# A two-layer trunk: the second input product of each feed-forward pair as seven products, with weight sums made by adding transfers

## The chip, the cores and the metric

The kernel runs on one core of a Trainium2 chip. The core has five engines with queues of their own: TensorE (PE, matmuls into PSUM), VectorE (DVE), ScalarE (ACT), GpSimd (POOL) and SyncE (SP, which here only issues transfers). Each queue runs in order; engines wait for each other by semaphores. 16 DMA engines move data between HBM and the on-chip buffer. The metric is the device time of one execution in microseconds (us). Before the change it is 1288.16 us, the median of 3 runs (1286.86 to 1289.29).

## The reference

A trunk of two layers on 512 tokens of width 1024, in float32. Each layer mixes tokens (layer 0: a gated linear recurrence beside stick-breaking attention; layer 1: a matrix memory) and then applies a convolutional gated feed-forward network, which is the part that matters here:

```python
def conv_glu_ffn(h, w_in, conv_w, conv_b, w_out):
    u = jnp.matmul(h, w_in)                  # 1024 -> 2 x 2816
    a, g = jnp.split(u, 2, axis=-1)
    a = causal_dwconv(a, conv_w, conv_b)     # 3 taps along the tokens
    return jnp.matmul(jax.nn.gelu(a) * g, w_out)   # 2816 -> 1024

# in each layer, around both sub-layers (mod = silu(c) @ ada_w + ada_b, six parts):
h = rmsnorm(x, norm_g) * (1 + scale) + shift
x = x + gate * sublayer(h)
```

## The kernel before

**Layout and precision.** Activations stand with channels on the 128 partitions and the 512 tokens along the row. A float32 operand is split into a high part, rounded to a faster matmul type (`hi`), and the rest (`lo`); a product is three matmuls, hi x hi, hi x lo and lo x hi (`mm3`, L254). Weights come by DMA as a `raw` tile; `split_w` (L219) makes `hi` with a cast on ScalarE (L222) and `lo` with a subtraction on VectorE (L223). Loads are issued by SP in order and wait there until a raw buffer is free.

**The feed-forward network** (`ffn`, L1130). The 2816 columns of either factor are 22 blocks of 128. Two pairs of blocks (fi = 0 and 2) are done first, plainly, while the second half of the normalised input is still being made. That half needs an inverse norm, computed by GpSimd (`rstd_of`, L336) and transposed by TensorE (L340). Then `tokens_side` makes combinations of token halves and channel halves, and nine **sets** follow, fi = 4, 6, ... 20, of two blocks each.

**A set.** The factor a ("X") is done by the class `Seven`: the weights of two blocks (1024 x 256) are seen as 2 x 2 blocks of 512 x 128, the input as 2 x 2 of 512 channels x 256 tokens, and Winograd's form of Strassen's scheme replaces eight block products by seven. Each product is 4 x 3 matmuls of 256 columns. Sums of the products are kept in PSUM where possible (products 1, 6, 7, 4 add up in one buffer, 5 and 3 in another, 2 in a third), and intermediate values are copied out after each. The sums of weights are four VectorE operations a set (L1083 to L1088). The factor g ("Y") is done plainly: two tiles of 8 x 3 matmuls of 512 columns. `ORDER` gives the order of these jobs, `FETCH` and `LEAD` how many jobs ahead loads and splits are called for. After the last job of a set, `post` applies convolution, gelu and the product of both factors, and splits the result into `acts`.

**Output products** are done in groups of 4 or 6 blocks of `acts`, put into the sets fi = 6, 10 and 14 and behind the last one (`out_jobs`); each output tile ends with an update of x on VectorE (L385). The last four blocks are multiplied at the end in two token halves.

**The conditioning** of layer 1 is 48 dot products on VectorE (L169, 1024 elements a row, with a 512 KB load each); 24 of them run in the network of layer 0, called for by `take`, two after each pair or set.

The Tile scheduler sets each engine's order from the program's order, the buffers and its own priorities.

## Time and profile before

| what | value |
|---|---|
| median of 3 runs | 1288.16 us |
| the profiled execution, device time | 1288.47 us |
| its span, first to last instruction | 1286.7 us |
| TensorE busy | 1246.4 us, 6942 matmuls seen |
| VectorE busy | 917.6 us |
| ScalarE busy | 578.9 us |
| GpSimd busy | 113.7 us |
| bytes moved | 161.04 MB |

Busy time is read per engine; matmuls are pipelined, so the printed durations of neighbouring matmuls overlap and their starts tell the spacing. A wait is put down to what ended it. Idle time of an engine that nobody waits for costs nothing. A few per cent of matmul records are missing from the trace, so counts of matmuls in a stretch are slightly low. In names, `wa` and `wg` are weights of the two factors, `was` sums of them, `wd` output weights, `pp`, `u` and `v` copies and sums of products, `th` and `tl` token combinations, `nr` the inverse norm, `acc` and `mx` PSUM buffers.

### The profile page before, as it was taken

To read this page: it belongs to the slowest core of one execution; us is meant where nothing else is said; L and a number is where in the kernel's file an instruction comes from. 1 tells how busy PE (TensorE), PEld (TensorE's weight loads), DVE (VectorE), ACT (ScalarE), POOL (GpSimd) and SP (SyncE) were. 2 spreads that over 40 slices of the span, in tenths; PEclk is the share of its full clock that TensorE was granted. 3 is DMA by queue.
4 is the path that set the end of the run, shared out by engine and by line. 5 is a ranking of instruction groups with operands and counts; after the bars stand their busy time and mean duration, and the time that the engine had idled before them with its cause. 6 is when DMAs were issued, how large, how long until landed. Compare 5 with 4: busy or idle time off the path is not lost.

```text
span 1286.7 us, 18103 instructions
## 1 busy us (share of the span) xinstructions
PE 1246.4 (97%) x6942; PEld 1060.2 (82%) x6942; DVE 917.6 (71%) x1503; ACT 578.9 (45%) x1011; POOL 113.7 (9%) x199
## 2 busy tenths in 40 slices
PE   5999999999989999999999999999999999999997
PEld 4876788899878888888897777778988888888887
DVE  7845788857876776768776869776797475657665
ACT  4454323235452434344446674774455152525432
POOL 0021254400000000000000120221000000000000
PEclk9999999999999999999999999999999999999999
DMA  8823655422434343435423338522232332323211
GB/s 319 296 70 99 220 171 178 135 83 67 147 99 148 120 141 118 140 119 181 136 80 115 98 100 267 157 66 67 66 115 75 106 114 83 112 85 111 86 49 66
DMA packets 47078, 161.04 MB, mean 125 GB/s; under 512 B 5136, under 2 KB 7568, under 8 KB 46992
## 3 DMA queue, kind: packets, MB, share of 16 engines
q1 hardware_dynamic: 46992, 159.89, 38.8%
q8 instruction: 54, 0.88, 0.3%
q14 instruction: 32, 0.26, 0.1%
HBM read 157.77 MB, written 2.10 MB: 124 GB/s over the span
## 4 chain that ended last, share of the span: by engine, by line
PE 86%; DVE 5%; issue 3%; ACT 3%; DMA 2%; POOL 1%; SPq 0%; POOLq 0%; DVEq 0%; ACTq 0%
PE acc L255 13%; PE acc L256 13%; PE acc L257 13%; PE mx L255 5%; PE mx L256 5%; PE mx L257 5%; PE acc L1107 4%; PE acc L1108 4%; PE acc L1109 4%; PE acc L657 2%; PE mx L488 2%; PE mx L659 2%; PE acc L289 1%; PE acc L291 1%; PE acc L290 1%
## 5 line engine op out<-in xcount | busy, mean ns | idle before, releaser
L255 PE MATMUL acc<-hh,wg 128*128 128x512 f32 (+1 forms) x384 | 144.0, 376 | 1.2 <-DVE cv L1148 1.2
L256 PE MATMUL acc<-hl,wg 128*128 128x512 f32 (+1 forms) x384 | 144.4, 376 | 0.0
L257 PE MATMUL acc<-hh,wg 128*128 128x512 f32 (+1 forms) x384 | 144.1, 376 | 0.0
L169 DVE CUSTOM_DVE_ANT_0 adaraw<-adaraw,csb,par 128x1024 f32<-128x1024 f32 x96 | 123.0, 1293 | 4.3 <-DMA adaraw<-adaT 4.2
L256 PE MATMUL mx<-actl,wd 128*128 128x512 f32 x288 | 113.5, 394 | 0.0
L255 PE MATMUL mx<-acth,wd 128*128 128x512 f32 x288 | 112.8, 395 | 0.0
L257 PE MATMUL mx<-acth,wd 128*128 128x512 f32 x288 | 112.1, 394 | 0.0
L255 PE MATMUL acc<-hh,w 128*128 128x512 f32 x256 | 105.6, 412 | 0.0
L222 ACT CAST w<-wraw 128x1024 fp32r<-128x1024 f32 x68 | 71.2, 1051 | 68.5 <-PE acc L256 35.0
L257 PE MATMUL acc<-hh,w 128*128 128x512 f32 x256 | 101.9, 398 | 0.0
L256 PE MATMUL acc<-hl,w 128*128 128x512 f32 x256 | 101.7, 397 | 0.0
L223 DVE TENSOR_TENSOR w<-wraw,w 128x1024 fp32r<-128x1024 f32 x68 | 83.5, 1234 | 24.3 <-ACT w L222 14.6
L1107 PE MATMUL acc<-th,wa 128*128 128x256 f32 x288 | 83.3, 289 | 4.9 <-ACT th L1187 3.5
L222 ACT CAST wg<-wgraw 128x1024 fp32r<-128x1024 f32 x44 | 46.1, 1048 | 86.5 <-PE acc L1108 64.6
L385 DVE SCALAR_TENSOR_TENSOR x<-mx,mod,x 128x512 f32<-128x512 f32 x64 | 47.8, 749 | 52.1 <-PE mx L257 51.7
L255 PEld LDWEIGHTS acc<-hh,wg 128*128 128x128 f32 x384 | 72.1, 188 | 14.8 <-ACT wa L222 1.4
L257 PEld LDWEIGHTS acc<-hh,wg 128*128 128x128 f32 x384 | 72.0, 188 | 13.7 <-DVE wg L223 0.4
L1108 PE MATMUL acc<-tl,wa 128*128 128x256 f32 x288 | 81.7, 284 | 1.1 <-DVE tl L1188 1.1
L256 PEld LDWEIGHTS acc<-hl,wg 128*128 128x128 f32 x384 | 72.1, 188 | 12.3
L1109 PE MATMUL acc<-th,wa 128*128 128x256 f32 x288 | 81.4, 283 | 0.0
L336 POOL TENSOR_TENSOR nr<-nv,mhalf 128x2 f32<-128x2 f32 (+1 forms) x9 | 7.7, 854 | 815.4 <-ACT nv L334 815.4
L222 ACT CAST wa<-was 128x1024 fp32r<-128x1024 f32 x36 | 37.8, 1050 | 69.1 <-PE mx L256 29.8
(307 smaller groups left out, 3254.9 us busy)
## 6 DMA issues: line engine op xcount, KB each, us to landing
adaraw<-adaT SPq DMA_DIRECT2D x96, 512.0 KB, 4.4
wraw<-wflat SPq DMA_DIRECT2D x76, 512.0 KB, 4.2
waraw<-wflat SPq DMA_DIRECT2D x44, 512.0 KB, 3.7
wgraw<-wflat SPq DMA_DIRECT2D x44, 512.0 KB, 4.4
wdraw<-wflat SPq DMA_DIRECT2D x32, 512.0 KB, 3.8
x<-xT SPq DMA_DIRECT2D x8, 256.0 KB, 4.6
wdraw<-wflat SPq DMA_DIRECT2D x8, 256.0 KB, 2.7
outT<-fin SPq DMA_DIRECT2D x6, 256.0 KB, 2.4
```

The source lines that it names most:

```text
L169: return nc.vector.tensor_tensor_reduce(out=tile_, in0=tile_, in1=csb, scale=1.0, scalar=pc("ada_b", o), op0=ALU.mult, op1=ALU.add, accum_ ...
L222: nc.scalar.copy(hi, src)
L223: nc.vector.tensor_sub(lo, src, hi.bitcast(F32))
L255: nc.tensor.matmul(out, ah, bh, start=start, stop=False)
L256: nc.tensor.matmul(out, ah, bl, start=False, stop=False)
L257: nc.tensor.matmul(out, al, bh, start=False, stop=stop)
L385: nc.vector.scalar_tensor_tensor(x[j][:, sl], ps, g, x[j][:, sl], op0=ALU.mult, op1=ALU.add)
L488: nc.tensor.matmul(lps[:, c * 64:(c + 1) * 64].rearrange("p (b m) -> p b m", m=m), k[:, s], qu, start=True, stop=True)
L657: nc.tensor.matmul(vps[i], act[:, i * P:(i + 1) * P], wt_[:, 0:512], start=s0, stop=s1)
L1107: nc.tensor.matmul(ps, hi[:, ks], bh, start=first and kk == 0, stop=False, skip_group_check=True)
L1108: nc.tensor.matmul(ps, hi[:, ks], bl, start=False, stop=False, skip_group_check=True)
L1109: nc.tensor.matmul(ps, lo[:, ks], bh, start=False, stop=kk == 3, skip_group_check=True)
```

## The change

Both factors of every set, in both networks, are done by `Seven` (`PAIRS`); jobs of X and Y alternate in the order `TWO`. The sums of weights are no longer made by VectorE: a tile is loaded with plain blocks by SP, and further blocks are added onto it by transfers with `accum_op=add` that GpSimd issues. Product 5's tile takes one such transfer of two blocks, product 6's takes three (one block, two, two), each after the one before. Signs are turned so that only additions are needed, and the token combinations and copies follow. Tiles of products 1, 5, 6 have two buffers of their own each (`raw`, `pr`, `qw`), shared by X and Y; product 4's block has smaller ones. Output groups are (0,4), (4,4), (8,4), (12,4), (16,2), placed after the fourth job of the sets fi = 4, 8, 12, 16 and behind the last; the other five sets have none. `tokens_side` is called before the first set instead of inside the pair fi = 2. A conditioning column is taken after each output tile of groups 1 to 4 and nowhere else.

```diff
-    NW, NR, NS, NQ, NX, NA = 45, 4, 10, 2, 2, 2
+    NW, NR, NS, NQ, NA = 44, 2, 10, 2, 2
...
+    def load_blocks(tile_, at, i0, n, add=False):
+        o, m = at + i0 * P * T, n * P * T
+        eng = nc.gpsimd if add else nc.sync
+        eng.dma_start(tile_.rearrange("p (b c) -> p b c", b=n),
+                      wflat[o:o + m].rearrange("(b p c) -> p b c", b=n, p=P),
+                      **({"accum_op": ALU.add} if add else {}))
...
-    ORDER = ("X1", "X5", "X6", "X2", "X7", "Y0", "X3", "X4", "Y1")
-    OUT_AT, LEAD, FETCH = 3, 6, 9
+    TWO = ("X1", "Y1", "X2", "Y2", "X5", "Y5", "X6", "Y6", "X3", "X7", "Y7", "Y3", "X4", "Y4")
+    LEAD, STAGE = 5, 3
+    PAIRS = (True, True)
...
-                nc.vector.tensor_add(src[:, 0:T], a21, a22)
-                nc.vector.tensor_sub(self.s2, src[:, 0:T], a11)
...
+            return {
+                1: [lambda: start(1, 0, 2)],
+                5: [lambda: add(5, 2), lambda: start(5, 1, 2)],
+                6: [lambda: load_blocks(t[6][:, 0:T], self.at, 3, 1, True), lambda: add(6, 2), lambda: add(6, 1),
+                    lambda: start(6, 0, 2)],
+                4: [lambda: start(4, 3, 1)],
+            }
         def prep(self, n):
...
+            hi, lo = split_w(self.t[n], self.name)
+            for i, m in enumerate({1: (2, 1), 5: (7, 5), 6: (3, 6), 4: (4,)}[n]):
...
-        groups = ((0, 6), (6, 4), (10, 4), (14, 4), (18, 4))
+        groups = ((0, 4), (4, 4), (8, 4), (12, 4), (16, 2), (18, 4))
...
                         x_update(ps, layer, 1, cb * (cols // P) + s)
+                        if gi > 0:
+                            take(1)
...
+            sevens = {"X": Seven(w, fi * P, bs, "wa")}
+            if two:
+                sevens["Y"] = Seven(w, F + fi * P, bs, "wg")
...
-            set_jobs(fi, {6: 0, 10: 1, 14: 2}.get(fi))
-        out_jobs(3)
+            set_jobs(fi, {4: 0, 8: 1, 12: 2, 16: 3}.get(fi))
+        out_jobs(4)
```

How the instructions stand, at three places.

GpSimd's queue at the start of layer 0's network, before: `nr` is the inverse norm of either token half, `hr` the last work of layer 0's mixer. The norm of the second half follows that of the first, and the next row is already layer 1's.

```order
L445 TENSOR_TENSOR hr_2256<-hr_2256,mhalf 128x4
L336 TENSOR_TENSOR nr_2592<-nv_2590,mhalf 128x2
L336 TENSOR_TENSOR nr_2795<-nv_2793,mhalf 128x2
L336 TENSOR_TENSOR nr_5956<-nv_5954,mhalf 128x2
L950 MEMSET vc_6142 128x4
```

The same place now. `waraw` and `wgraw` from `wflat` are adding transfers, X's and Y's; the brackets name the queues waited for, DMAHW a load's landing, DMASW an add's.

```order
L459 TENSOR_TENSOR hr_2256<-hr_2256,mhalf 128x4 [waits Pool_49]
L350 TENSOR_TENSOR nr_2592<-nv_2590,mhalf 128x2 [waits Activation_49]
L206 DMA waraw_3145<-wflat 128x2x512 [waits DMAHW2_49,DMAHW4_49,DMAHW0_49,DMAHW6_49,DVE_49,Activation_49]
L206 DMA waraw_3140<-wflat 128x2x512 [waits DMAHW5_49,DMAHW7_49,DMAHW0_49,DVE_49]
L350 TENSOR_TENSOR nr_2799<-nv_2797,mhalf 128x2 [waits Activation_49]
L206 DMA waraw_3140<-wflat 128x2x512 [waits DMASW1_49]
L206 DMA waraw_3140<-wflat 128x512 [waits DMASW2_49]
L206 DMA wgraw_3148<-wflat 128x2x512 [waits DMAHW7_49,DMAHW1_49,DVE_49]
L206 DMA wgraw_3142<-wflat 128x2x512 [waits DMAHW2_49,DMAHW0_49,DVE_49]
L206 DMA wgraw_3142<-wflat 128x2x512 [waits DMASW5_49]
```

Two adding transfers now stand ahead of the second half's norm; in layer 1's network it is one.

GpSimd's queue for one set, fi = 10, now (before, it had nothing between the norms): tiles 4194 and 4210 are product 5's of X and Y, 4102 and 4144 product 6's.

```order
L206 DMA waraw_4194<-wflat 128x2x512 [waits DMAHW4_49,DMASW0_49,DVE_49]
L206 DMA wgraw_4210<-wflat 128x2x512 [waits DMAHW7_49,DMASW1_49,DVE_49]
L206 DMA waraw_4102<-wflat 128x2x512 [waits DMAHW2_49,DMASW5_49,DVE_49]
L206 DMA waraw_4102<-wflat 128x2x512 [waits DMASW2_49]
L206 DMA wgraw_4144<-wflat 128x2x512 [waits DMAHW5_49,DMASW7_49,DVE_49]
L206 DMA waraw_4102<-wflat 128x512 [waits DMASW3_49]
L206 DMA wgraw_4144<-wflat 128x2x512 [waits DMASW4_49]
L206 DMA wgraw_4144<-wflat 128x512 [waits DMASW6_49]
```

The third add of X (one block) stands behind Y's first and its own second; each of the four last rows waits for the landing of an earlier add.

VectorE's queue among the first output tiles of a group in layer 0, before, in set fi = 6: `x` rows end an output tile, L223 rows are `lo` parts of splits, ISA rows are conditioning columns.

```order
L385 SCALAR_TENSOR_TENSOR x_78<-mx_3549,mod,x_78 128x512
L223 TENSOR_TENSOR wd_3423<-wdraw_3420,wd_3422 128x1024
L385 SCALAR_TENSOR_TENSOR x_79<-mx_3569,mod,x_79 128x512
L223 TENSOR_TENSOR wd_3474<-wdraw_3471,wd_3473 128x1024
L223 TENSOR_TENSOR wd_3429<-wdraw_3426,wd_3428 128x512
L169 ISA adaraw_3445,mod<-adaraw_3445,csb,par 128x1024
L169 ISA mod 128x1
L169 ISA adaraw_3448,mod<-adaraw_3448,csb,par 128x1024
L169 ISA mod 128x1
L385 SCALAR_TENSOR_TENSOR x_80<-mx_3589,mod,x_80 128x512
L223 TENSOR_TENSOR wd_3501<-wdraw_3498,wd_3500 128x1024
L223 TENSOR_TENSOR wd_3480<-wdraw_3477,wd_3479 128x512
```

The same kind of place now, in set fi = 8: `waraw_3759` is the tile of X6 (L237 is the old L223, L399 the old L385).

```order
L399 SCALAR_TENSOR_TENSOR x_80<-mx_4030,mod,x_80 128x512
L169 ISA adaraw_4044,mod<-adaraw_4044,csb,par 128x1024
L169 ISA mod 128x1
L399 SCALAR_TENSOR_TENSOR x_81<-mx_4047,mod,x_81 128x512
L169 ISA adaraw_4061,mod<-adaraw_4061,csb,par 128x1024
L169 ISA mod 128x1
L237 TENSOR_TENSOR wa_4065<-waraw_3759,wa_4064 128x1024
L399 SCALAR_TENSOR_TENSOR x_82<-mx_4068,mod,x_82 128x512
L169 ISA adaraw_4082,mod<-adaraw_4082,csb,par 128x1024
L169 ISA mod 128x1
L399 SCALAR_TENSOR_TENSOR x_83<-mx_4085,mod,x_83 128x512
L169 ISA adaraw_4099,mod<-adaraw_4099,csb,par 128x1024
```

A column now follows each output tile, and X6's split, which frees that tile's buffer for the next set, stands behind the fourth of eight output tiles.

## Rows read from the trace of the kernel before

**Rows 1.** page, first part: busy us (share of span) xinstructions by engine

```profile
PE 1246.4 (97%) x6942; PEld 1060.2 (82%) x6942; DVE 917.6 (71%) x1503; ACT 578.9 (45%) x1011; POOL 113.7 (9%) x199
```

**Rows 2.** windows: us, busy us (instructions) by engine, clock, DMA share, GB/s

```profile
400.00:500.00 100.00, 100.00 (x554) 86.12 (x553) 69.37 (x95) 38.04 (x52) 0.00 (x0) 1.00 0.40 130
1195.70:1217.60 21.90, 21.90 (x136) 19.58 (x135) 13.82 (x18) 10.57 (x17) 0.00 (x0) 1.00 0.34 103
```

**Rows 3.** timeline, TensorE: start, us, engine, line, operation; ends of two runs

```profile
500.05 0.39 PE L257 MATMUL acc<-hh,wg 128*128 128x512 f32 x1
...
504.48 0.39 PE L255 MATMUL acc<-hh,wg 128*128 128x512 f32 x1
...
507.81 0.28 PE L1108 MATMUL acc<-tl,wa 128*128 128x256 f32 x1
...
508.98 0.28 PE L1109 MATMUL acc<-th,wa 128*128 128x256 f32 x1
```

**Rows 4.** timeline, ScalarE: copies of first products, sets 18 and 20

```profile
590.93 0.37 ACT L1113 COPY pp<-acc 128x256 f32<-128x256 f32 x1
...
612.07 0.37 ACT L1113 COPY pp<-acc 128x256 f32<-128x256 f32 x1 [0.17 <-PE acc L256]
```

**Rows 5.** groups by line: shapes xcount | busy us, mean ns | idle before

```profile
L169 DVE CUSTOM_DVE_ANT_0 adaraw<-adaraw,csb,par 128x1024 f32<-128x1024 f32 x96 | 123.0, 1293 | 4.3 <-DMA adaraw<-adaT 4.2
L223 DVE TENSOR_TENSOR wa<-was,wa 128x1024 fp32r<-128x1024 f32 x36 | 44.0, 1223 | 21.1 <-ACT wa L222 20.5
L223 DVE TENSOR_TENSOR wa<-waraw,wa 128x512 fp32r<-128x512 f32 x18 | 12.3, 685 | 0.0
L385 DVE SCALAR_TENSOR_TENSOR x<-mx,mod,x 128x512 f32<-128x512 f32 x64 | 47.8, 749 | 52.1 <-PE mx L257 51.7
L1121 DVE TENSOR_TENSOR v<-mx,pp 128x256 f32<-128x256 f32 x18 | 7.5, 418 | 1.3 <-PE acc L1109 1.2
L222 ACT CAST wg<-wgraw 128x1024 fp32r<-128x1024 f32 x44 | 46.1, 1048 | 86.5 <-PE acc L1108 64.6 <-PE acc L256 20.7 <-PE mx L1108 0.6
L1113 ACT COPY pp<-acc 128x256 f32<-128x256 f32 x18 | 6.6, 367 | 0.9 <-DVE actl L251 0.8 <-PE acc L256 0.2
```

**Rows 6.** TensorE's waits, 300:660 and 910:1287: total us, times, longest

```profile
PE acc L1107 <- ACT th L1187: 3.5, 1, 3.5
PE acc L1108 <- DVE tl L1188: 0.3, 1, 0.3
...
PE mx L340 <- POOL nr L336: 1.1, 1, 1.1
PE acc L1108 <- DVE tl L1188: 0.8, 1, 0.8
PE acc L1107 <- ACT pp L1113: 0.5, 1, 0.5
```

**Rows 7.** timelines, GpSimd and VectorE, norms at both networks' start

```profile
308.89 0.70 POOL L336 TENSOR_TENSOR nr<-nv,mhalf 128x2 f32<-128x2 f32 x1 [16.53 <-ACT nv L334]
...
922.34 0.70 POOL L336 TENSOR_TENSOR nr<-nv,mhalf 128x2 f32<-128x2 f32 x1 [17.94 <-ACT nv L334]
...
304.03 1.22 DVE L223 TENSOR_TENSOR wa<-waraw,wa 128x1024 fp32r<-128x1024 f32 x1
```

**Rows 8.** DMA, 5:30, then 400:600: GB/s by slice, issues, us to landing

```profile
GB/s 302 311 318 377 387 400 403 429 419 419 419 419 419 419 419 413 406 413 413 400 400 413 413 419 197 92 229 374 243 157 315 302 203 328 282 236 334 354 354 380
DMA packets 2774, 8.71 MB, mean 348 GB/s; under 512 B 308, under 2 KB 308, under 8 KB 2774
q1 hardware_dynamic: 2774, 8.71, 94.7%
...
wraw<-wflat SPq DMA_DIRECT2D x4, 512.0 KB, 6.3
...
wgraw<-wflat SPq DMA_DIRECT2D x14, 512.0 KB, 4.7
waraw<-wflat SPq DMA_DIRECT2D x12, 512.0 KB, 3.7
```

More of the change, by code (lines that the diff above doesn't have):

```diff
@@ new lines, in tokens_side @@
+            uh, u, vh, v = (wt(n, [P, 2, 256], dt=F32R) for n in ("th", "tl", "th", "tl"))
+            nc.scalar.copy(uh[:, 0, :], uf[:, 0, :])
+            nc.scalar.activation(uh[:, 1, :], uf[:, 1, :], AF.Identity, bias=ns)
+            nc.vector.tensor_sub(u[:, 0, :], uf[:, 0, :], uh[:, 0, :].bitcast(F32))
+            nc.vector.scalar_tensor_tensor(u[:, 1, :], uf[:, 1, :], ns, uh[:, 1, :].bitcast(F32), op0=ALU.add,
+                                           op1=ALU.subtract)
+            nc.scalar.copy(vh, vf)
@@ L1248, in post @@
             def post():
-                take(2)
                 for s in range(2):
-                    act_g(act_a(fi + s, first.v[s]), st[s])
-            order = FIRST if fi == 4 else ORDER
+                    act_g(act_a(fi + s, sevens["X"].v[s]), sevens["Y"].v[s] if two else st[s])
+            order = TWO if two else ONE_FIRST if fi == 4 else ONE
+            out_at = 4 if two else 3
+            base = len(jobs)
+            pos = {name: i for i, name in enumerate(order)}
             for i, name in enumerate(order):
-                if i == OUT_AT and outs is not None:
+                if i == out_at and outs is not None:
@@ L1256, in set_jobs @@
                     out_jobs(outs)
                 n = int(name[1])
-                p = PREPS[i] if i < len(PREPS) else None
                 prep = None
-                if p:
-                    prep = second_prep if p[0] == "Y" else lambda n=int(p[1]): first.prep(n)
-                jobs.append((first.fetch if i == 0 else None, prep,
-                             (lambda n=n: first.run(n)) if name[0] == "X" else lambda n=n: second(n),
-                             post if i == len(order) - 1 else None))
@@ L1266, in ffn @@
-        for fi in range(4, NF, 2):
-            set_jobs(fi, {6: 0, 10: 1, 14: 2}.get(fi))
-        out_jobs(3)
-        nf = npr = 0
-        for j, (_, _, run, post) in enumerate(jobs):
-            while nf < min(j + FETCH, len(jobs)):
-                if jobs[nf][0]:
-                    jobs[nf][0]()
-                nf += 1
+                if name[0] in sevens:
+                    sev = sevens[name[0]]
+                    if n in (1, 5, 6, 4):
+                        prep = seven_at(sev, n, len(jobs))
+                    run = lambda sev=sev, n=n: sev.run(n)
+                else:
+                    if n == 0:
+                        prep = second_prep
+                    run = lambda n=n: second(n)
@@ L1275, in ffn, with advance @@
+                jobs.append((prep, run, post if i == len(order) - 1 else None))
+        for fi in range(4, NF, 2):
+            set_jobs(fi, {4: 0, 8: 1, 12: 2, 16: 3}.get(fi))
+        out_jobs(4)
+        fetches.sort(key=lambda e: e[:2])
+        npr = 0
+        def advance(j):
+            nonlocal npr
+            while fetches and fetches[0][0] <= j:
+                fetches.pop(0)[2]()
             while npr < min(j + LEAD, len(jobs)):
-                if jobs[npr][1]:
-                    jobs[npr][1]()
+                if jobs[npr][0]:
+                    jobs[npr][0]()
@@ L1278, in ffn @@
                 npr += 1
+        for j, (_, run, post) in enumerate(jobs):
+            advance(j)
+            if j == 0:
+                for kk in range(4):
+                    tokens_side(kk)
             run()
```

123 lines of the change are left out of this document (65 added, 58 removed).

## The prediction

> **What bounds the kernel now.** The page comes first: TensorE is busy for 97% of a span of 1286.7 us, VectorE for 71%, ScalarE for 45%, GpSimd for 9% [rows 1]. A busy TensorE alone proves little, so the windows are read next. In 100 us of the first feed-forward network, and in a set of the second, TensorE shows no gap at the full clock (1.00, the 2.4 GHz level), while the DMA engines are busy for 0.40 and 0.34 of the time [rows 2]. The list of TensorE's waits closes it: from the norm of either network's input to its end the longest are 3.5 us, once, for the token combinations, and 1.1 us, once, for the norm [rows 6]. So in these stages the time is the number of matmuls times their spacing, as long as everything else stays hidden.
>
> The spacing is read from starts, since the printed durations overlap. With 512 columns, 20 consecutive starts run from 500.05 to 504.48: 4.43 us over 19 steps, 0.233 us each. With 256 columns, 11 starts run from 507.81 to 508.98: 0.117 us each [rows 3]. Halving the columns halves the step; the weight loads do not set a floor there. As a check, a set of two column pairs without output products goes from 590.93 to 612.07, 21.14 us [rows 4]; 48 x 0.233 + 84 x 0.117 is 21.0.
>
> **What the change takes away.** Each of 18 sets (nine in either network) did its second factor in 48 matmuls of 512 columns, 11.2 us; it now does seven products of 12 matmuls of 256, 84 x 0.117 = 9.83 us, or 9.95 if the 0.14 us that my sum is short in the set is put on the sevens. I take 9.9: a gain of 1.29 us a set, 23.2 us for 18. All of it is on the path. The token combinations are now needed only after the first two pairs of products and a group of output products (four jobs of 5.6 us, two tiles of 12 matmuls of 0.233), so the waits of 3.5, 0.3 and 0.8 us for them go: 4.6 us [rows 6]. The four VectorE sums of each old set were hidden under the matmuls and give no time back by themselves. The 24 conditioning columns stay in the first network, each now behind one output tile. There TensorE takes 2.8 us for a tile and VectorE 0.75 us to add it and 1.29 for a column [rows 5], 2.04 us; a split or two beside them is covered by the sets' loads being due later. I take nothing; without that cover it would be the columns' excess, 24 x 0.5 us at the most.
>
> **What it adds on VectorE and ScalarE.** A set without output products lasts 2 x 9.9 = 19.8 us now. Between 1195.7 and 1217.6 VectorE was busy for 13.8 us and ScalarE for 10.6 [rows 2]. Splitting fourteen blocks of 512 columns instead of nine costs VectorE 8.7 us (6 x 1.223 + 2 x 0.685) where it had 5.6, and three more product evictions cost 3 x 0.42 [rows 5]: 18.2 us of 19.8, 92%. ScalarE gets one wide and one narrow cast more and four evictions of 0.37: 13.7 us, 69%. Both still fit, but these queues run in order, and the slack of an eviction is short: the next set's first product takes the buffer whose last product was one job (1.4 us) earlier, and a cast of 1.05 us can stand in front of the copy of 0.37. In the old order the slack was as short in places (the product after X5 waits for X1's copy), and the second network's nine sets waited 0.5 us for such copies [rows 6]. So the cost lies between nothing and one such wait of 1.2 us a set, 22 us; nearest to the rows is a fraction, and with the fuller queues I take 0.3 us a set, 5 us in all.
>
> **What it adds at the start of each network.** GpSimd computes the inverse norms; in the first network it does so at 308.89 and in the second at 922.34, and TensorE waits 1.1 us for the latter [rows 6, 7]. Now two adding transfers stand in front of it in GpSimd's queue in the first network and one in the second, each waiting for a load whose buffer VectorE frees with a split such as those that end by about 305.3 [rows 7]. A load then lands 3.7 to 4.7 us later [rows 8], near 309.5, so the norm starts some 1 to 3 us late; TensorE's transposes of it, and with them all that it has queued behind, wait. Between nothing and two whole landings (9 us), I take 3 us for both networks.
>
> **What it adds to the transfers.** This is the term that no row shows: there is no adding transfer before. A block is 128 x 512 numbers, 0.262 MB. A seven loads seven blocks and adds seven, in four adding transfers; it loaded four before. X6's chain is one load, two adds of 0.52 MB and one of half that, each after the one before it has landed, and Y6's runs beside it, interleaved on GpSimd's queue. The tile of X6 is freed by its split in the fourth of eight output tiles, 11.2 us before the set goes on; the next set's split is due after ten more products less two, so 11.2 + 11.3 = 22.5 us later if that set has no output products. Five of nine sets are like that; the others have some 39 us. With a load of 4.2 us [rows 8] and L for an add, a shorter one at L - 1, X6 is ready at 4.2 + 3L - 1, which allows L up to 6.4 us. Y6's load starts two output tiles (5.6 us) later and its split is due at about 26 us: 9.8 + 3L - 1, so L up to 5.7. From below L is 3.7 us, a plain load; from above 12.6, two passes of the 6.3 us that a load takes when the engines are full [rows 8]. I take 5.5: a plain load of 4.2 us and 1.3 us for a second pass of 0.52 MB at the 400 GB/s of a full stretch. That leaves 0.6 us in each of ten sets; with some spread I take 3 us in all. The first set is loaded during 45 us of earlier products.
>
> **The sum.** The profiled execution took 1288.47 us around its span of 1286.7; the median of the three runs is 1288.16, so it stands for them. -23.2 - 4.6 + 5 + 3 + 3 = -16.8 us: 1271.7, and I predict 1272 us. What belongs to this case alone is 1262 (no stall at all, 1288.5 - 27.8 = 1260.7, and a little left) to 1278 (evictions 11 us instead of 5).
>
> **Rival on the other side: adds that pass their bytes twice fill the DMA engines.** Nine sets of 19.8 us and output products for eighteen rows of weights at 5.6 us make 279 us, 31.0 us a set. A set moves 3.67 MB of loads, 3.67 of adds, 1.05 of output weights and, in the first network, 1.4 of conditioning rows: 9.8 and 8.4 MB, 316 and 271 GB/s. Counting adds double it is 13.5 and 12.1 MB, 435 and 390 GB/s. The fullest stretch moved 348 GB/s at a share of 94.7%, that is 368 at all of it, with whole slices above 400 [rows 8]. At 368 a set takes 36.7 and 32.9 us, 5.7 and 1.9 too long, 68 us over 18 sets; at 410 it is 32.9 and 31.0, 17 us. So 1289 to 1340, middle 1310, and slower as soon as more than 17 us is lost. Against it: at one pass the same engines have room in both networks. For it: an add has two operands to fetch where a load has one, and no row says that the second comes free.
>
> The Trainium skill, Collectives: The Full Stack, section The bandwidth ceiling, states this of a reduction between cores: it runs at half a copy's rate not because the addition is slow but because two sources are read through the same ring. By that rule this rival would be the result. No run here shows it yet for an add that ends in the state buffer.
>
> **Rival between: only the chain is late.** L is 6.3 to 7.2 us, for GpSimd's time to issue a transfer or its queue held by one late landing. Y6 is then 1.8 to 4.5 us late in ten sets; some 2 us of it pass unseen, since its products come two or more jobs after the split: 0 to 25 us, on average 11, in place of the 3 above: 1280 (1278 to 1290). The rest of the gain shows, but TensorE has a regular gap in the sets without output products. GpSimd is idle in the networks, which speaks against a long writing time; four landings in series on one queue speak for it.
>
> **Rival: no gain in the matmuls.** If the sevens ran at the weight load's pace TensorE would gain nothing; the 0.117 us of the old sevens [rows 3] says no, and I give it no chance of its own.
>
> **How the numbers follow.** The forecast's case 52%, the late chain 20%, full DMA engines 25%, and 3% for faster than 1262. About 0.2% (2.6 us) is what a measurement tells from no change, so faster means below 1285.6: 52 + 3 and half of the late chain, 65%; same 8% (the end of the late chain and the start of the full engines); slower 27%. The range takes the late chain whole and half of the full engines: 1262 to 1312.
>
> **What would show it.** Right: matmul steps of 0.117 us through whole sets without output products, some 20 us from set to set; TensorE's share in the networks at 98% or more; adds that land within 6 us; VectorE near 90% in such sets. Wrong in the last terms: casts of the X6 and Y6 tiles on ScalarE waiting for a DMA, and TensorE idle behind evictions queued after them; DMA share near 1.0 through the first network but not the second (full engines), or moderate shares with long landings (late chain); a norm at the start of a network that waits for GpSimd's queue. If the sets take 20 us and the time still does not fall, the loss is at the start of the networks or in a stage that the change does not name, and the forecast's picture is wrong.

## The result, and the profile after

The changed kernel takes **1436.49 us** (median of 4 runs, 1433.98 to 1440.57): 1.1155 times the kernel before, with an interval of 1.1137 to 1.1172. The forecast was 1272. The profiled execution has a span of 1438.9 us. First its busy line, which answers to [rows 1]:

```profile
PE 1264.2 (88%) x7590; PEld 1105.0 (77%) x7590; DVE 932.4 (65%) x1537; ACT 630.4 (44%) x1123; POOL 278.4 (19%) x343
```

TensorE's idle time, span less busy, was 1286.7 - 1246.4 = 40.3 us and is 174.7 now. Its busy time should have fallen by the 23 us that the matmuls are worth and has risen by 17.8. So some 134 us are waits, and some 40 us are matmuls at a lower clock (e7 below has the same number of matmuls, busy for 1225.2 us at a clock of 1.00). The windows show both (us, busy us of PE, PEld, DVE, ACT and POOL, granted clock, DMA share, GB/s), the first one against the same stretch in [rows 2]:

```profile
400.00:500.00 100.00, 81.39 (x528) 74.98 (x529) 61.84 (x86) 39.10 (x64) 22.82 (x20) 0.89 0.95 236
470.00:480.00 10.00, 2.33 (x18) 2.12 (x18) 3.47 (x5) 0.20 (x1) 2.30 (x3) 0.86 1.05 283
480.00:490.00 10.00, 4.06 (x19) 4.06 (x20) 3.18 (x4) 2.48 (x4) 1.69 (x3) 0.50 0.87 201
560.00:570.00 10.00, 0.00 (x0) 0.00 (x0) 0.00 (x0) 0.00 (x0) 2.10 (x2) 0.63 0.94 221
570.00:580.00 10.00, 8.21 (x52) 8.21 (x53) 5.52 (x8) 5.49 (x9) 4.60 (x4) 0.69 0.91 174
```

The DMA share is 0.95 where it was 0.40. In 560:570 no engine but GpSimd does anything, and GpSimd only issues adds: the kernel waits for transfers. After such a gap TensorE comes back at a lower clock: 0.50, its 1.2 GHz level, in 480:490, and 0.69 in 570:580. Who waits for what is in the lists of waits (total us, times, longest). TensorE's, in the first and in the second network:

```profile
PE acc L1125 <- ACT wg L236: 66.3, 8, 14.0
...
PE acc L1125 <- ACT wg L236: 45.0, 8, 9.2
```

ScalarE's, over the whole span:

```profile
ACT wa L236 <- DMA waraw<-wflat: 107.9, 10, 15.6
```

TensorE's 111.3 us are waits for casts of the second factor's tiles, ScalarE's 107.9 us waits of casts of the first factor's for transfers. One such place in ScalarE's timeline (start, us, engine, line, operation, idle time before it):

```profile
570.17 1.04 ACT L236 CAST wa<-waraw 128x1024 fp32r<-128x1024 f32 x1 [14.93 <-DMA waraw<-wflat]
571.12 0.61 ACT L236 CAST wg<-wgraw 128x512 fp32r<-128x512 f32 x1
```

And in TensorE's:

```profile
571.79 0.58 PE L1125 MATMUL acc<-th,wg 128*128 128x256 f32 x1 [13.84 <-ACT wg L236]
```

In ScalarE's order the narrow cast (Y4, the last product of the running set) stands right behind the cast of the tile with three adds, X6 of the next set. ScalarE stops for X6, and TensorE for Y4, whose own tile is a plain load. The transfers over the sets of the first network, 340:700, with queue totals (packets, MB, share of 16 engines) and medians from issue to landing, against [rows 8]:

```profile
q0 software_dynamic: 15616, 29.88, 49.5%
q1 hardware_dynamic: 21270, 51.41, 41.9%
...
wgraw<-wflat POOLq DMA_DIRECT2D x25, 512.0 KB, 9.1
waraw<-wflat SPq DMA_DIRECT2D x24, 512.0 KB, 5.5
wgraw<-wflat SPq DMA_DIRECT2D x24, 512.0 KB, 8.4
waraw<-wflat POOLq DMA_DIRECT2D x24, 512.0 KB, 9.0
```

q0 carries the adds: 58% of the bytes of q1 in more engine time. On the page of the whole execution, the second row being the adds:

```profile
q1 hardware_dynamic: 70608, 188.21, 39.3%
q0 software_dynamic: 34560, 66.07, 27.5%
```

188.21 MB in 39.3% of 16 x 1438.9 us is 20.8 GB/s an engine, 333 on all; 66.07 MB in 27.5% is 10.4, or 167. Per byte, an add takes about twice the engine time of a load. The matmuls themselves keep the forecast's step; ten starts of TensorE in the changed kernel, 496.29 to 497.36, are nine steps of 0.119 us against 0.117 in [rows 3]:

```profile
496.29 0.28 PE L1127 MATMUL acc<-th,wg 128*128 128x256 f32 x1
...
497.36 0.28 PE L1127 MATMUL acc<-th,wg 128*128 128x256 f32 x1
```

And GpSimd at the start of the first network, where [rows 7] had the inverse norm at 308.89:

```profile
306.05 1.41 POOL L206 DMA_DIRECT2D waraw<-wflat  x1 [14.08 <-DVE hraw L392]
308.47 1.21 POOL L206 DMA_DIRECT2D waraw<-wflat  x1 [1.01 <-DVE hl L395]
309.24 1.19 POOL L350 TENSOR_TENSOR nr<-nv,mhalf 128x2 f32<-128x2 f32 x1
```

Two adds stand in front of it now, and it comes 0.35 us later.

### The profile page after: what moved, and what is told of

The parts are those of the page before. It is cut to its first block, busy times and chain, and to the rows that moved or that the text cites. A ratio compares the mean times of both kernels' runs of the same rounds, so it can differ in the third digit from the quotient of the medians.

```text
span 1438.9 us, 20091 instructions
## 1 busy us (share of the span) xinstructions
PE 1264.2 (88%) x7590; PEld 1105.0 (77%) x7590; DVE 932.4 (65%) x1537; ACT 630.4 (44%) x1123; POOL 278.4 (19%) x343
## 3 DMA queue, kind: packets, MB, share of 16 engines
q1 hardware_dynamic: 70608, 188.21, 39.3%
q0 software_dynamic: 34560, 66.07, 27.5%
## 4 chain that ended last, share of the span: by engine, by line
PE 48%; DMA 22%; DVE 11%; issue 10%; ACT 5%; POOL 3%; SPq 0%; POOLq 0%; DVEq 0%; ACTq 0%
DMA waraw<-wflat 7%; PE acc L269 7%; PE acc L270 7%; PE acc L271 7%; DMA wdraw<-wflat 7%; DMA wgraw<-wflat 6%; PE acc L1125 2%; PE mx L269 2%; DMA adaraw<-adaT 2%; PE mx L270 2%; PE acc L1127 2%; PE mx L271 2%; PE acc L1126 2%; PE mx L502 2%; PE acc L671 2%
## 5 line engine op out<-in xcount | busy, mean ns | idle before, releaser
L1125 PE MATMUL acc<-th,wg 128*128 128x256 f32 x288 | 88.2, 306 | 111.3 <-ACT wg L236 111.3
L236 ACT CAST wa<-waraw 128x1024 fp32r<-128x1024 f32 (+1 forms) x80 | 76.1, 952 | 211.1 <-DMA waraw<-wflat 107.9
L237 DVE TENSOR_TENSOR wa<-waraw,wa 128x1024 fp32r<-128x1024 f32 (+1 forms) x80 | 88.1, 1101 | 121.9 <-ACT wa L236 121.0
L206 POOL DMA_DIRECT2D waraw<-wflat x72 | 92.2, 1284 | 379.2 <-DMA waraw<-wflat 257.0
L1125 PEld LDWEIGHTS acc<-th,wg 128*128 128x128 f32 x288 | 59.0, 205 | 115.4 <-ACT wg L236 115.4
L206 POOL DMA_DIRECT2D wgraw<-wflat x72 | 95.9, 1332 | 248.1 <-DMA wgraw<-wflat 226.2
L169 DVE CUSTOM_DVE_ANT_0 adaraw<-adaraw,csb,par 128x1024 f32<-128x1024 f32 x96 | 123.8, 1294 | 26.1 <-DMA adaraw<-adaT 25.8
L269 PE MATMUL mx<-acth,wd 128*128 128x512 f32 x288 | 116.6, 408 | 8.6 <-ACT acth L264 5.5
L236 ACT CAST wg<-wgraw 128x1024 fp32r<-128x1024 f32 (+1 forms) x80 | 76.1, 952 | 74.4 <-PE mx L270 46.5
L269 PE MATMUL acc<-hh,w 128*128 128x512 f32 x256 | 105.2, 411 | 0.0
L237 DVE TENSOR_TENSOR wg<-wgraw,wg 128x1024 fp32r<-128x1024 f32 (+1 forms) x80 | 88.0, 1100 | 16.0 <-ACT wg L236 13.2
L237 DVE TENSOR_TENSOR w<-wraw,w 128x1024 fp32r<-128x1024 f32 x68 | 83.5, 1234 | 20.4 <-ACT w L236 10.9
L1127 PE MATMUL acc<-th,wg 128*128 128x256 f32 x288 | 85.2, 296 | 1.7 <-DVE wg L237 1.7
L1126 PE MATMUL acc<-tl,wg 128*128 128x256 f32 x288 | 85.2, 296 | 0.0
L399 DVE SCALAR_TENSOR_TENSOR x<-mx,mod,x 128x512 f32<-128x512 f32 x80 | 59.3, 748 | 38.6 <-PE mx L271 38.5
```

The costliest lines, as they stand in the source:

```text
L169: return nc.vector.tensor_tensor_reduce(out=tile_, in0=tile_, in1=csb, scale=1.0, scalar=pc("ada_b", o), op0=ALU.mult, op1=ALU.add, accum_ ...
L206: eng.dma_start(tile_.rearrange("p (b c) -> p b c", b=n), wflat[o:o + m].rearrange("(b p c) -> p b c", b=n, p=P), **({"accum_op": ALU.add} ...
L236: nc.scalar.copy(hi, src)
L237: nc.vector.tensor_sub(lo, src, hi.bitcast(F32))
L269: nc.tensor.matmul(out, ah, bh, start=start, stop=False)
L399: nc.vector.scalar_tensor_tensor(x[j][:, sl], ps, g, x[j][:, sl], op0=ALU.mult, op1=ALU.add)
```

## The experiments

The networks' times below run from the start of the inverse norm at a network's input to that of the first one after it, both on GpSimd. The forecast came to some 11 us less than before in the first and 8 in the second.

```
                                         us    ratio (interval)        1st net  2nd net
before                                 1288.2                           350.5    344.2
after                                  1436.5  1.1155 (1.1137-1.1172)   437.6    410.1
e1  adds as plain transfers            1332.6  1.0359 (1.0338-1.0380)   389.0    349.4
e2  adds of half the columns           1368.5  1.0638 (1.0613-1.0663)   391.8    379.3
e4  one seven, sums by adds            1300.5  1.0113 (1.0078-1.0148)   355.0    356.7
e6  one add a seven, VectorE the rest  1317.7  1.0246 (1.0229-1.0264)   368.1    353.3
e7  no sums                            1262.9  0.9810 (0.9796-0.9825)   336.5    334.7
e8  conditioning as before             1456.6  1.1296 (1.1268-1.1325)   456.5    409.0
e9  e6, second factor's by GpSimd      1362.6  1.0570 (1.0540-1.0599)   394.2    376.5
e10 e6, outputs meant to be even       1330.2  1.0329 (1.0313-1.0344)   378.9    357.5
e11 after, outputs meant to be even    1430.1  1.1088 (1.1052-1.1123)   439.6    394.0
e12 all sums on VectorE                1311.2  1.0178 (1.0163-1.0194)   362.4    353.9
e13 e12 in the second network alone    1291.9  1.0026 (1.0014-1.0038)   342.9    359.1
e14 one seven, all sums on VectorE     1279.8  0.9931 (0.9918-0.9945)   342.9    343.1
e15 e7, adds aside                     1546.0  1.2000 (1.1950-1.2050)   486.2    466.4
e16 e7, plain transfers aside          1415.5  1.0987 (1.0891-1.1083)   414.0    402.1
e18 after, product 4's tile elsewhere  1472.5  1.1445 (1.1419-1.1471)   450.8    422.5
```

**e1, e2: the adds' time on the engines.** e1 issues the same 144 transfers into the same tiles without the addition (the sums are left out); e2 adds half of the columns of each (half of the sums are left out).

```diff
-                      **({"accum_op": ALU.add} if add else {}))
+                      )
```

> The adding transfers are issued by GpSimd as plain transfers onto the same tiles (same count, size, queue and waits; the weight sums are left out). Theory A (an add takes two passes of the DMA engines, 10.4 GB/s an engine against 20.8, so the engines are full): a set then needs 29 us of the engines in the first network and 25 in the second, both under 31, so nearly all of the loss goes: 1270 to 1290 us, software queue's share near 14% instead of 27.5%. Theory B (the serial chain on GpSimd's queue is late whatever a transfer does): landings fall from 8 to some 5 us, but the queue's order stays and the sets stay long: above 1330 us.

> Each adding transfer moves only half of its columns (rows of 1 KB instead of 2; half of each weight sum is left out); count, order and waits as before. Theory A (bytes): the adds need 11 to 14 us of the engines a set instead of 22, so 25 to 32 us a set against 31: 1275 to 1310 us. Theory B (number of landings in series): the chain has as many landings, each 2 us or so of fixed time and most of the queueing kept, so the time stays above 1370 us.

The queue of these transfers in e1, then in e2:

```profile
q0 software_dynamic: 18432, 66.07, 14.7%
```

```profile
q0 software_dynamic: 34560, 33.04, 16.4%
```

In e1 the same bytes take 3131 engine-us, 21.1 GB/s an engine, in place of 6331, and 104 of the 148 us lost against the kernel before come back. So the doubled engine time, with what hangs on it, is most of the loss. (e1 also doubles the size of a packet and shortens GpSimd's issues, see the last section; no run takes these apart from the addition.) But it is not all: by its total e1 lies where theory B put it, above 1330 us, and 70 us above e7 below, which has no such transfers. Its landings (KB each, median us) and TensorE's wait for the second factor's casts:

```profile
waraw<-wflat POOLq DMA_DIRECT2D x54, 512.0 KB, 4.9
wgraw<-wflat POOLq DMA_DIRECT2D x54, 512.0 KB, 5.8
```

```profile
PE acc L1125 <- ACT wg L236: 34.5, 10, 10.6
```

The second network is nearly that of before (349.4); the first, where the conditioning loads come on top, is not. e2 lies between its two theories, just under B's 1370 us. It halves the bytes, but the packets stay as many, and one takes 0.104 us for 1 KB where an add of 2 KB took 0.183: halving a packet does not halve its time. Why e2's second network is 30 us behind e1's, at 3580 engine-us against 3131, is open; GpSimd's issues are as long in e2 as in the changed kernel (1.26 to 1.30 us), in e1 half that.

**e7: no sums at all.** Both factors as sevens in the new order with the new evictions; product 6 takes product 5's tile (the sums are left out).

```diff
-                5: [lambda: add(5, 2), lambda: start(5, 1, 2)],
-                6: [lambda: load_blocks(t[6][:, 0:T], self.at, 3, 1, True), lambda: add(6, 2), lambda: add(6, 1),
-                    lambda: start(6, 0, 2)],
+                5: [lambda: start(5, 2, 2)],
+                6: [lambda: same(6, 5)],
```

> Both factors as seven products, in the order and with the evictions of the change, but without any sum of weights: product 5 takes the second pair of blocks as it lies in memory, product 6 the same tile, so no adding transfer is issued and 5 blocks are loaded per seven where the changed kernel loads 7 and adds 7 (the sums are left out of the computation). Theory (the loss is in making the sums): with the sums gone the forecast's other terms must show, -23 us for matmuls, -5 for token combinations, +5 for evictions: 1262 to 1275 us, sets of 24 us without and 41 us with output products in both networks, no long wait of TensorE for a cast. Rival (the sevens themselves cost more than forecast, in splits on VectorE, evictions or buffers): 1285 us or more, with waits of TensorE on VectorE or ScalarE, not on transfers.

1262.93 us, at the lower end. Its busy line:

```profile
PE 1225.2 (97%) x7590; PEld 1075.9 (85%) x7590; DVE 932.2 (74%) x1537; ACT 630.2 (50%) x1123; POOL 114.3 (9%) x199
```

A window inside each network, as above:

```profile
400.00:590.00 190.00, 188.32 (x1295) 173.65 (x1294) 154.48 (x217) 93.36 (x144) 0.00 (x0) 1.00 0.58 183
1020.00:1210.00 190.00, 189.61 (x1319) 175.45 (x1318) 127.15 (x169) 93.66 (x147) 0.00 (x0) 1.00 0.34 110
```

ScalarE's copies of the first products of three sets:

```profile
398.02 0.64 ACT L1133 COPY pp<-acc 128x256 f32<-128x256 f32 x2
420.12 0.64 ACT L1133 COPY pp<-acc 128x256 f32<-128x256 f32 x2
461.65 0.64 ACT L1133 COPY pp<-acc 128x256 f32<-128x256 f32 x2
```

Busy time falls by 21.2 us (forecast 23.2 for the matmuls), idle time by 4.5; sets take 22.1 and 41.5 us at the full clock. All of the forecast but the sums is there. What is left, 1436.5 - 1262.9 = 174 us, is the price of making sums by adding transfers, with the two further blocks that each seven loads for them; the forecast had 3 us for it, and 3 for the norm behind the adds. Of the 174 us 104 go in e1 and 70 stay.

**e8: the conditioning columns as before**, two behind each pair and set instead of one behind an output tile.

```diff
                         x_update(ps, layer, 1, cb * (cols // P) + s)
-                        if gi > 0:
-                            take(1)
...
             def post():
+                take(2)
```

> The changed kernel with one part undone: the conditioning columns of the first network are taken as before (two behind each of the first tile pairs and behind each set) instead of one behind each output tile. Theory (transfer engines full): the conditioning bytes are the same, so the first network still lasts about 437 us and the whole 1425 to 1445 us. Rival (order of the queue: each conditioning load stands in SyncE's queue in front of weight loads and waits for its buffer there): the first network comes down toward the second's 410 us, the whole to 1405 to 1420 us.

Both missed: the first network gets slower by 19 us, the second stays. The change's placement is itself a gain where transfers are short; it is not part of the loss.

**e4, e6, e9, e12: the sums elsewhere.** e4 keeps the plain second factor (PAIRS is False twice) and makes one factor's sums by adds. e6 keeps both sevens and the adding transfer for product 5; product 6's sum is two VectorE additions. In e9 the second factor's two are GpSimd's; in e12 there is no adding transfer, and VectorE makes all sums.

```diff
             if n == 6:
+                t = self.t
+                s = t[6] = raw_tile(self.name + "s", D, "qw")
+                nc.vector.tensor_add(s, t[1], t[5])
+                nc.vector.tensor_add(s[:, 0:T], s[:, 0:T], t[4])
```

> The second factor again plainly, in 48 matmuls of 512 columns; the first factor's seven products with sums by adding transfers, the new groups and the new place of the conditioning columns stay. Theory A: per set 5.3 MB of plain loads and 1.84 MB of adds, 27 us of the engines in the first network, 23 in the second, of 32.3: it fits, so the time is that of before within a few us, 1285 to 1295. Theory B: one chain of four landings a set instead of two interleaved; by it too the sets fit, unless sets without output products (21 us) are late: 1290 to 1310.

> Both factors as seven products, but only product 5's sums by an adding transfer (one a seven instead of four); product 6's sums by two VectorE additions from the tiles of products 1, 5 and 4, which stay longer. Theory A: 5.1 MB of loads and 1.05 MB of adds a set, 21 us of the engines in the first network and 17 in the second, of 31: the engines have room, and the matmul gain of 23 us shows unless VectorE (3.8 us more a set) is the next bound: 1268 to 1290. Theory B: the chain is one landing long: the same, 1268 to 1290. If it stays far above 1290, what costs is neither the bytes nor the chain but the sevens themselves.

> The version in which only product 5's sums are made by an adding transfer and product 6's by two vector additions (1317.7 us), with the second factor's two additions on GpSimd instead of VectorE. If VectorE's share (81% in the first network, 68% in the second, and 17 us of TensorE's waits end on its split of the first factor) is what is left: 36 x 0.95 = 34 us off VectorE, TensorE's waits for it fall from 26 us toward 10 and the time to 1298 to 1308 us. If the queue order of loads and adding transfers is what is left, or GpSimd's additions (by the rows of 256 columns some 4 + 2 us a set) delay the adding transfers behind them: 1315 to 1330 us.

> Both factors as seven products in the change's order, but every sum of weights made by VectorE (four additions of 512 or two of 512 and one of 1024 columns a seven, 3.3 us) from the four blocks that each seven loads; no adding transfer at all. Without any sum the kernel takes 1262.9 us. VectorE gets 36 x 3.3 = 117 us more (932 to about 1050 us), and in a set without output products 18.2 + 6.6 = 24.8 us of work where the products take 19.8. Theory (the loss is the adding transfers' time on the transfer engines and the chain behind them; VectorE has the room on average): 1270 to 1295 us, below the 1317.7 us of the version with one adding transfer a seven. Rival (VectorE's bursts in the sets without output products bind, some 5 us late in each of ten sets and the clock lost behind each gap): 1305 us or more.

e4 halves the adds and keeps the matmuls of before, and is still 12 us slower than before: above what theory A allowed, inside B's range. e6 and e12 land between: 119 and 125 us better than the changed kernel, 30 and 23 worse than before. e6 misses both its theories (1268 to 1290 us); that the sevens themselves cost so much, which it names for that case, e7 rules out. Windows over the sets, e6 and then e12:

```profile
310.00:636.00 326.00, 304.08 (x2006) 277.90 (x2005) 261.98 (x374) 150.88 (x231) 20.86 (x18) 0.97 0.61 169
```

```profile
310.00:636.00 326.00, 308.36 (x2017) 278.88 (x2017) 285.79 (x415) 151.43 (x239) 0.69 (x1) 0.97 0.37 123
```

and TensorE's longest sum of waits in e12:

```profile
PE acc L1137 <- DVE wg L237: 16.1, 12, 2.0
```

In e12, with a DMA share of 0.37, VectorE is the late one: 88% busy over the window (80% in e6), and TensorE waits for its splits. e12's total is in its rival's range: the 25 us that e7 gains do not pay for VectorE's sums. e9 loses 45 us more than e6, outside both its ranges. Its GpSimd additions, and the wide and narrow splits of the first factor on VectorE beside them:

```profile
L1114 POOL TENSOR_TENSOR wgs<-wgraw,wgraw 128x1024 f32<-128x1024 f32 x18 | 52.9, 2939 | 259.3 <-DVE wd L237 139.0 <-ACT wa L236 55.1 <-DVE wg L237 26.3
...
L237 DVE TENSOR_TENSOR wa<-waraw,wa 128x1024 fp32r<-128x1024 f32 x44 | 57.9, 1317 | 0.5
L237 DVE TENSOR_TENSOR wa<-waraw,wa 128x512 fp32r<-128x512 f32 x18 | 17.7, 985 | 0.1
```

The narrow split takes 985 ns where it takes 685 [rows 5]: GpSimd's additions slow the engine that they were to relieve, and the adding transfers stand behind them in GpSimd's queue. What either costs of the 45 us is not separated.

**e10, e11: output products spread evenly.**

```diff
-            set_jobs(fi, {4: 0, 8: 1, 12: 2, 16: 3}.get(fi))
+            set_jobs(fi, {f: ((f - 4) // 4, (f - 4) // 2 % 2) for f in range(4, 20, 2)}.get(fi))
```

> The version with product 5's sums by one adding transfer and product 6's by two vector additions (1317.7 us), with the output products spread evenly: half a group behind every set instead of a whole group behind every second one, so a set is some 31 us throughout instead of 24 and 41 to 50. Theory (the limit is the rate of transfers and splits in the stretches without output products, since their mean over two sets is below TensorE's time: DMA share 0.66 and 0.52, VectorE 81% and 68%): TensorE's waits of 26 us and the clock lost behind them nearly vanish, 1270 to 1290 us, so at or below the kernel before. Rival (a chain of loads, adds and splits per set that is too long wherever it stands, or buffers held longer by the spread): 1305 us or more.

> The changed kernel with the output products spread evenly behind all sets in the same way. Theory (an add takes the transfer engines twice as long per byte, and the mean over two sets needs 40.4 us of them in the first network and 36.2 in the second where the products need 31): evening helps little, sets of 38 to 44 us throughout, 1400 to 1440 us. Rival (the series of four adding transfers is only late where a set without output products gives it 20 us): with 31 us for every set it fits (4.2 + 3 x 8 = 28 us), and the time falls to 1300 to 1350 us.

Neither tells anything of its question, though e10 lands in its rival's range and e11 in its theory's. First copies of three sets in e11:

```profile
417.53 0.64 ACT L1131 COPY pp<-acc 128x256 f32<-128x256 f32 x2
...
443.31 0.64 ACT L1131 COPY pp<-acc 128x256 f32<-128x256 f32 x2
...
504.02 0.64 ACT L1131 COPY pp<-acc 128x256 f32<-128x256 f32 x2
```

25.8 and 60.7 us: the sets are as uneven as they were, since TensorE got the output products of two sets nearly in one block whatever the order in the code: of their first matmuls (L269) 6 stand in the shorter stretch and 26 in the longer one, in e11 as in the changed kernel.

**e15, e16: the transfers without anyone who waits.** The kernel of e7, and beside it the changed kernel's adds (e16: plain transfers) into two tiles that nothing reads, with the load that starts each tile, from GpSimd's queue too. The sums stay left out.

```diff
-                5: [lambda: start(5, 2, 2)],
-                6: [lambda: same(6, 5)],
+                5: [lambda: add(9, 2), lambda: start(5, 2, 2)],
+                6: [lambda: (same(6, 5), load_blocks(t[9][:, 0:T], self.at, 3, 1, True)), lambda: add(9, 2),
+                    lambda: add(9, 1), lambda: start(9, 0, 2)],
```

> The version without sums (1262.9 us; six sets from the second to the eighth take 190.5 us in the first network and 189.0 in the second, in the changed kernel 259.5 and 235.6), with the changed kernel's adding transfers put back beside it: for every seven the same four adds (and the load that starts their tile, from GpSimd's queue too) go into a tile that nothing reads, so no product, load or split waits for an add; the two tiles for them turn on GpSimd's queue alone. The sums still don't enter the computation. Read from the pace of the sets, since GpSimd's late queue may hold the norm behind the network. Theory (the adds' time on the transfer engines makes the weight loads late): at the same bytes the six sets take 215 to 260 us with TensorE waiting for casts of loads, DMA share over 0.9. Rival (only the series of adds that a split waits for is late): the six sets stay at 189 to 197 us.

> The same with the transfers aside issued as plain ones, which take half the engine time per byte: both theories expect the six sets near 190 us (189 to 200); if they are as slow as with adds, it is the number of transfers and not their time on the engines that counts.

The six sets and the total can't be used: GpSimd's queue falls behind, and once in each network an output-weight load waits for it, some 120 us in e15. Before that stall there are two whole sets to read. e15's copies of first products:

```profile
408.06 0.64 ACT L1134 COPY pp<-acc 128x256 f32<-128x256 f32 x2
434.24 0.64 ACT L1134 COPY pp<-acc 128x256 f32<-128x256 f32 x2
483.29 0.64 ACT L1134 COPY pp<-acc 128x256 f32<-128x256 f32 x2
```

The window over them:

```profile
404.00:478.00 74.00, 66.91 (x424) 60.38 (x423) 50.44 (x71) 29.80 (x48) 18.45 (x17) 0.93 0.99 262
```

Landings of SyncE's loads in it (KB each, median us):

```profile
wgraw<-wflat SPq DMA_DIRECT2D x4, 512.0 KB, 7.9
...
waraw<-wflat SPq DMA_DIRECT2D x4, 512.0 KB, 8.9
```

The same loads in e7, 398:472:

```profile
waraw<-wflat SPq DMA_DIRECT2D x4, 512.0 KB, 4.7
wgraw<-wflat SPq DMA_DIRECT2D x4, 512.0 KB, 3.7
```

With nothing waiting for an add, the loads still land twice as late, and the pair of sets takes 75.2 us against 63.6 in e7 and 85.4 in the changed kernel (413.17 to 498.59). So in that pair 11.6 of 21.8 us come with traffic that nobody waits for. In the second network, before the stall, the same pair takes 67.0 us against 62.8 in e7 and 78.9 in the changed kernel: 4.2 of 16.1. The rest is then what waits for the adds. e16's pairs take 73.0 us at a share of 0.87 and 67.0 us, hardly less or no less, so its expectation missed. By its own words that speaks for the number of transfers and against their time on the engines, as far as the harm goes that they do from aside; the engine time shows where something waits for the transfers (e1). With two sets of each network, this is an indication of the split, no more.

**e18: another place in ScalarE's queue.** The transfers stay; Y4's tile takes a wide buffer and is cast ahead of the next set's X6.

```diff
-        if n <= T:
+        if n <= T and name != "wg":
             return tuple(wsp.tile([P, T], F32R, tag="wq", name=nm(name), bufs=NQ)[:, :n] for _ in range(2))
```

> The changed kernel with one buffer changed: the second factor's narrow tile (product 4) takes a wide weight buffer in place of the only narrow pair, which it had to get from the first factor's. In ScalarE's order its cast then stands well ahead of the cast of the next set's tile for X6, where it stood right behind it, so TensorE's last product of a set no longer waits for three adds that belong to the next set. Theory (queue order turns the late adds into waits about six products, 8 us, before they are needed): the 111 us of waits for that cast mostly go and the whole falls to 1360 to 1400 us. Rival (the engines are full, so the lateness only moves to the next cast): waits of the same sum stand behind the casts of X6 and Y6, and the whole stays at 1415 to 1440 us, since six sets need 242 and 217 us of the transfer engines against 259 and 236 measured.

TensorE's waits over the span:

```profile
PE acc L1125 <- ACT pp L1131: 93.5, 10, 12.6
PE mx L269 <- ACT acth L264: 37.6, 8, 7.4
PE acc L1125 <- ACT v L1147: 24.5, 6, 7.4
```

The wait for Y4's cast is gone, and 156 us of waits stand behind the copies and casts that come next in ScalarE's queue. The theory is wrong. The rival has the lateness moving on, as it does, but not to the casts that it named, and 1472.5 us lies above its range: the order decides which instruction shows the lateness, not that there is some. Transfers take 0.89 of the time in 340:700, as before this edit (0.92).

**e13, e14: back to one seven.** e13 is e12 with both factors as sevens in the second network alone; e14 has one seven in both networks, with all sums on VectorE.

```diff
-    PAIRS = (True, True)
+    PAIRS = (False, False)
```

> As before, with both factors as sevens in the second network alone, where no conditioning columns load VectorE (71% there without sums, against 79% in the first); in the first network the second factor is a plain product as in the kernel before, and all sums are VectorE's. If the first network then lasts as before (350.5 us less up to 4 for the token combinations) and the second gains what VectorE's room allows (344.2 down to 335 to 342): 1275 to 1286 us, the first version to beat the kernel before. If VectorE's bursts bind in the second network too: 1288 to 1300 us.

> The change's order without its two costly parts: one factor as seven products and the other plain, as in the kernel before, in both networks; all sums on VectorE; the new groups of output products, the later token combinations and the conditioning columns behind output products stay. In the version with this form in the first network alone that network took 342.9 us where the kernel before took 350.5. Theory (those smaller parts of the change gain by themselves: the token combinations' waits, 4.6 us, and shorter waits on splits and conditioning): the second network, which has no conditioning columns, gains 3 to 6 us, and the whole is 1273 to 1279 us. Rival (the first network's gain is all in the conditioning columns): the second network stays at 344 us, 1280 to 1282 us.

e13 is a little slower than before: its first network gains 7.6 us, its second loses 15. e14 is **the version that beats both kernels**, 1279.8 us, 0.9931 (0.9918 to 0.9945), so by 0.7%. Of its gain in the networks 7.7 us stand in the first and 1.1 in the second, so e14's rival is nearer: the second network hardly gains. In the first, the 3.5 us wait for token combinations [rows 6] is gone, and with it a lower clock. A window there in the kernel before, then in e14:

```profile
360.00:370.00 10.00, 6.12 (x33) 5.55 (x32) 8.88 (x16) 4.06 (x7) 0.00 (x0) 0.83 0.18 42
```

```profile
360.00:370.00 10.00, 10.00 (x45) 8.08 (x44) 10.00 (x18) 3.83 (x7) 0.00 (x0) 1.00 0.00 0
```

Over that network TensorE's idle time falls by 3.8 us and its busy time, with the same matmuls, by 3.2. That is most of the gain; nothing in it needs the conditioning columns.

e14 also tells what the second seven is worth where no transfer is late: TensorE is busy for 1242.8 us in it and for 1225.2 in e7, 17.6 us less.

## Why the prediction was wrong

**Right in the main: the matmuls, the token combinations, the evictions, the norm.** The forecast without its transfer term is 1269 us, without the norm's too 1266; e7 took 1262.9. That it is so near is in part luck, since errors cancel. The matmuls give some 17.6 us (e14 to e7) where 23.2 were taken: in e7's six sets from the second to the eighth a matmul of 256 columns takes 0.12 us on average, and the 0.117 came from eleven starts. The token combinations give more than 4.6 us, with the lower clock behind their wait. Idle time is 4.5 us less than before, where -4.6 for token combinations and +5 for evictions were expected, so the evictions cost less. The norm of the first network comes 0.35 us later and takes 1.19 instead of 0.70 us: under 1 us, where 3 for both networks was taken.

**Wrong: the term "+3 late adds", with L = 5.5 us.** What failed first is L, taken as a load and 1.3 us more. It measured 9.0 us in 340:700. With that, X6 is ready 5.5 + 3 x 9.0 - 1 = 31.5 us after its tile is freed, against the 22.5 of the prediction, 9.0 us late, and the first network's eight waits are 8.3 us each. L lies inside the bounds given (3.7 to 12.6), but the upper one was never carried into the time. The step from L to the time failed as well: in e1 L is about what the forecast took (4.9 and 5.8 us over the execution, 5.5 and 6.4 in 340:650), so by its sum X6 is on time and Y6 two or three us late a set, 30 us in all at the most, and e1 is 70 us above e7. Why is open, since no run takes the queue in which GpSimd issues the transfers apart from their traffic. Three things were missing:

- An add takes twice a load's engine time: 10.4 against 20.8 GB/s an engine. The Trainium skill's rule (Collectives: The Full Stack, section The bandwidth ceiling), two sources through one ring, gives this factor for a reduction between cores; e1 and the page's q0 row show 2.0 here, for an add into the state buffer.
- So the engines are nearly full (0.92 in 340:700), and the plain loads are late as well: 4.7 us became 8.4 for the second factor's [rows 8].
- The gaps bring a lower clock behind them. That is some 40 of the 152 us of span, and no step of the forecast had it.

**The rival "full engines" had the mechanism and too small a price.** It counted the engines at 368 to 410 GB/s; at the measured 333 and 167 a set needs 6.12/0.333 + 3.67/0.167 = 40.4 us in the first network and 36.2 in the second, six sets 242 and 217. From the second to the eighth set the changed kernel took 259.5 and 235.6 us, e7 190.5 and 189.0. The DMA share over these six sets, 0.96 and 0.93, bears the sum out. So the engines' need alone accounts for about 52 of 69 and 28 of 47 us; the rest, late series and the clock, is not separated. But room on the average is not enough either: the same sum gives e1 29 us a set in the first network and 25 in the second, under the 31 of the products, and yet e1's six sets take 231.5 and 200.2 us, 41 and 11 more than e7's. The rival's 25% should have been the larger chance, since no row spoke for the second operand being free. The rival "only the chain is late" had L too small too (6.3 to 7.2), and with it 1278 to 1290 us.

## What to carry to other kernels

Price a new kind of transfer by engine time (bytes by its own rate, summed over a stage, against the stage's compute time) before its latency, because once the engines were full here the plain loads of the stage were late too. Room on the average does not make it safe: e1 had it and lost 70 us. And a gap on TensorE cost more than its length here: the matmuls behind it ran at a lower clock.

## What was not expected of the hardware

- Adding transfers come in packets about half as large (34560 for 66.07 MB, against 18432 in e1), and GpSimd takes 1.28 to 1.33 us to issue one, against 0.68 to 0.69 for the plain one in e1.
- The clock behind gaps: 0.50 in 480:490 after 7.7 us without matmuls in the ten before, 0.69 in 570:580 after 10 us without any.
- A GpSimd addition of 128 x 1024 takes 2.94 us and VectorE's narrow split beside it 985 ns instead of 685. The Trainium skill (GPSIMD Engine Reference, section Architecture) has GpSimd's read and write ports shared with VectorE; e9 agrees.
